# A two-layer trunk kernel on one core: the low parts of the weights by an adding DMA

## The chip, the core and the metric

The kernel runs on one core of a Trainium2 chip. The metric is the device time of one execution in microseconds (us). Before the change the median of three runs is 747.53 us (746.16 to 750.75). One further execution was profiled; all rows below come from it.

## The reference

A batch of one, 512 positions and a width of 1024 go through two layers in float32. Layer 0 (even) normalises, multiplies by one wide input matrix, and splits the result into a gated chunked MLP, a differential attention of 8 heads and a cross-attention into 256 memory tokens; an output matrix brings the concatenation back to 1024, and it is added to the input. Layer 1 (odd) has the same frame around a convolution of 31 taps, a sparse attention of three branches and a second memory attention:

```python
def even_layer(x, ...):
    h = rms_norm(x, norm_g)
    a_u, a_v, a_g, b_q, b_k, b_v, b_g, m_q, m_g = split_cols(h @ w_in, EVEN_SPLITS)
    y_a = chunked_sgu(jax.nn.gelu(a_u), jax.nn.gelu(a_v), ...) * jax.nn.silu(a_g)
    y_b = o_b.reshape(Bz, S, B_WIDTH) * jax.nn.silu(b_g)
    y_m = memory_attention(m_q, mem_n, ...) * jax.nn.silu(m_g)
    return x + jnp.concatenate([y_a, y_b, y_m], axis=-1) @ w_out
```

## The kernel before, in words

**Products in three parts.** Every large product is made of float32r operands. An operand is split into a high part `h`, the value as float32r holds it, and a low part `l`, the float32 value less `h`. `mm3` (L395 to L398) adds three products: high by high (L396), high by low (L397), low by high (L398). In `proj_T` the weights are the stationary operand and their low part comes third; in `proj_N` the weights are the moving operand and their low part comes second.

**Weight units.** The large weights lie in HBM as 88 units of 128 x 1024 float32 (512 KB), and a 2240-column matrix is read in three more pieces. `load_unit` (L379) takes one page `u` of 2048 words from the pool of weight pages (kind "w" of `arena_r`), and a raw page of 1024 words (three exist); SyncE issues the load (L384), ScalarE copies raw to `h` (L376), and GpSimd subtracts, raw less `h`, into `l` (L377). The raw page comes free after the subtraction. Only the first four units of the program are given VectorE as the subtracting engine (L750, argument `eng`); the other 87 pieces use GpSimd. The same `split` helper with VectorE as default also makes high and low parts of activations, so L376 and L377 have ScalarE and VectorE instructions of other work as well.

**Pages.** There are five weight pages in the dense stages and fewer later (`W_OUT` is 4, `W_ATTN1` is 2, and free pages are lent between weights and activations). The copy into a page waits until TensorE has done the last product that read it. Pages are dealt out in program order.

**Order of work.** The program is written as streams (Python generators) that `merge` (L702) interleaves in given shares: attention with projections, gates, convolution taps and output products. A planner (`schedule_with_timeline_sim=True`, L1387) then sets the order in which each engine gets its instructions, by its own estimate of durations and by priority. On the chip each engine works through its own list in order, and waits on semaphores. GpSimd's list also holds the inverse square roots of the norms (`rstd`, L370 and L372), the scaling of some softmax rows (L570) and the additions of one convolution tile (L1257). VectorE's list holds the other three convolution tiles (L1259), score reductions (L925), softmax scaling (L572), norm arithmetic (L511, L883, L957) and the low parts of activations (L377).

Of the kernel before, what the change touches and what calls it, by code (L numbers as in the profile page):

```python
# [26 lines left out]
AF = mybir.ActivationFunctionType  # L27
ALU = mybir.AluOpType
AX = mybir.AxisListType
ADD, SUB, MUL, MAX = ALU.add, ALU.subtract, ALU.mult, ALU.max  # L30
# [255 lines left out]
def emit(ctx, tc, nc, D, out):  # L286
# [8 lines left out]
    def SC():  # L295
        return Scope(arenas)
# [8 lines left out]
    V, A, G, mm = nc.vector, nc.scalar, nc.gpsimd, nc.tensor.matmul  # L305
    dma = nc.sync.dma_start
    act = A.activation

    def f32(t):
        return t.bitcast(F32)  # L310
# [64 lines left out]
    def split(src, h, l, eng=None):  # L375
        act(h, src, AF.Copy)  # L376
        (eng or V).tensor_tensor(l, src, f32(h), SUB)  # L377

    def load_unit(sc, dram, w=DM, eng=None):  # L379
        u = sc([P, 2, DM], F32R, "w")  # L380
        h, l = u[:, 0, :w], u[:, 1, :w]
        with SC() as rs:
            raw = rs([P, w], F32, "raw")
            dma(raw, dram)  # L384
            split(raw, h, l, eng or G)
        return h, l

    def load(sc, name):
        i, n = UIDX[name]
        return [load_unit(sc, D["wall"][i + j]) for j in range(n)]  # L390
# [41 lines left out]
    def unit_parts(wsc, part, n, eng=None):  # L432
        w = []
        for nk, src in part:
            h, l = load_unit(wsc, src, nk * n, eng)
            w += [(h[:, j * n:(j + 1) * n], l[:, j * n:(j + 1) * n]) for j in range(nk)]
        return w
# [959 lines left out]
```

## Time and profile before

| what | value |
|---|---|
| median of three runs | 747.53 us (746.16 to 750.75) |
| the profiled execution | 751.36 us, span of its instructions 749.7 us |
| TensorE products, busy | 683.0 us (91%) |
| VectorE, busy | 533.0 us (71%) |
| GpSimd, busy | 390.3 us (52%) |
| ScalarE, busy | 365.9 us (49%) |
| mean granted TensorE clock | 0.959 of full speed |
| read from HBM | 57.46 MB |

The span is the time from the first to the last instruction; 1.7 us of the profiled execution lie around it. Busy time of an engine that others do not wait for costs nothing. TensorE's products are pipelined, so that their busy times overlap a little, and 91% is not a peak rate.

### The profile page before, as it was taken

The numbers are of one execution on the slowest core, as the hardware profiler recorded it, in microseconds if no ns is written. First come the engines' busy times: TensorE is split into PE (matmuls) and PEld (weight loads), VectorE is DVE, ScalarE is ACT, GpSimd is POOL, SyncE is SP. The second block draws the span as 40 slices with busy tenths as digits, with TensorE's granted clock in tenths as the row PEclk, the third lists the DMA queues.
The fourth block names the chain that finished last, engine by engine and source line by source line (L and its number), as shares of the span: only waits on it lengthen the run. The fifth ranks groups of instructions, "written<-read, shape, count | busy, mean of one in ns | idle before, by whom it ended". The sixth has DMA issues, their size and how long they took to land.

```text
span 749.7 us, 10913 instructions
## 1 busy us (share of the span) xinstructions
PE 683.0 (91%) x3819; PEld 577.0 (77%) x3819; DVE 533.0 (71%) x1216; ACT 365.9 (49%) x819; POOL 390.3 (52%) x343
## 2 busy tenths in 40 slices
PE   4999999999999889999999799895579989899997
PEld 3889998778898668887887688684457878787866
DVE  4507798678778696745479829999636875979883
ACT  5245346465655674534254754322412745675651
POOL 3376985645356686417375586983233422442540
PEclk9999999999999998999999899998598999999999
DMA  8442244552222542112232110032021100110112
GB/s 304 156 150 75 65 145 118 167 161 92 71 85 86 180 154 108 66 57 66 80 126 73 56 57 29 29 115 83 0 84 57 57 29 29 57 57 30 57 66 75
DMA packets 22375, 66.55 MB, mean 89 GB/s; under 512 B 3504, under 2 KB 3760, under 8 KB 22320
## 3 DMA queue, kind: packets, MB, share of 16 engines
q1 hardware_dynamic: 22320, 65.86, 26.8%
q8 instruction: 30, 0.49, 0.3%
q14 instruction: 25, 0.20, 0.1%
HBM read 57.46 MB, written 2.10 MB: 79 GB/s over the span
## 4 chain that ended last, share of the span: by engine, by line
PE 60%; DVE 27%; POOL 4%; issue 4%; ACT 4%; DMA 1%; SPq 0%; ACTq 0%; DVEq 0%; POOLq 0%
PE banks L397 15%; PE banks L396 15%; PE banks L398 15%; DVE banks L1259 5%; PE banks L393 4%; DVE arena_r L377 4%; PE banks L923 2%; PE banks L1211 2%; POOL arena_f L372 2%; DVE arena_f L572 2%; POOL arena_r L377 2%; DVE arena_f L925 2%; ACT arena_r L376 2%; DMA arena_f<-in_wall_dram 1%; PE banks L961 1%
## 5 line engine op out<-in xcount | busy, mean ns | idle before, releaser
L396 PE MATMUL banks<-arena_r 128*128 128x512 f32 (+2 forms) x784 | 295.1, 382 | 11.3 <-DVE arena_f L473 3.3
L397 PE MATMUL banks<-arena_r 128*128 128x512 f32 (+2 forms) x784 | 295.3, 378 | 5.9 <-POOL arena_r L377 5.1
L377 POOL TENSOR_TENSOR arena_r<-arena_f,arena_r 128x1024 fp32r<-128x1024 f32 (+2 forms) x87 | 211.9, 2444 | 170.6 <-ACT arena_r L376 170.1
L398 PE MATMUL banks<-arena_r 128*128 128x512 f32 (+2 forms) x784 | 294.0, 377 | 0.0
L396 PEld LDWEIGHTS banks<-arena_r 128*128 128x128 f32 x784 | 151.9, 194 | 37.8 <-ACT arena_r L376 4.6
L397 PEld LDWEIGHTS banks<-arena_r 128*128 128x128 f32 x784 | 152.8, 195 | 31.0 <-POOL arena_r L377 6.6
L398 PEld LDWEIGHTS banks<-arena_r 128*128 128x128 f32 x784 | 152.4, 194 | 23.8 <-POOL arena_r L377 0.4
L376 ACT ACTIVATE arena_r<-arena_f 128x1024 fp32r<-128x1024 f32 (+2 forms) x131 | 110.3, 854 | 97.9 <-PE banks L398 31.8
L393 PE MATMUL banks<-const,arena_f 128*128 128x128 f32 x507 | 84.8, 286 | 34.1 <-DVE arena_f L521 12.4
L393 PEld LDWEIGHTS banks<-const,arena_f 128*128 128x128 f32 x507 | 63.6, 148 | 46.8 <-DVE arena_f L521 13.5
L376 ACT ACTIVATE arena_r<-banks 128x512 fp32r<-128x512 f32 (+1 forms) x112 | 57.9, 533 | 68.0 <-PE banks L393 42.9
L377 DVE TENSOR_TENSOR arena_r<-banks,arena_r 128x512 fp32r<-128x512 f32 (+1 forms) x112 | 67.2, 607 | 29.5 <-ACT arena_r L376 28.9
L925 DVE CUSTOM_DVE_ANT_0 arena_f<-banks,const 128x512 f32<-128x512 f32 (+3 forms) x128 | 60.4, 482 | 17.9 <-PE banks L923 14.0
L372 POOL TENSOR_TENSOR arena_f<-arena_f,const 128x4 f32<-128x4 f32 (+3 forms) x60 | 68.4, 1142 | 3.7
L570 POOL TENSOR_SCALAR arena_f<-arena_f 128x256 f32<-128x256 f32 (+3 forms) x48 | 30.8, 646 | 73.1 <-DVE arena_f L1190 27.6
L1259 DVE SCALAR_TENSOR_TENSOR banks<-arena_f,const,banks 128x482 f32<-128x482 f32 (+14 forms) x90 | 66.0, 733 | 1.5
L954 ACT ACTIVATE arena_f<-arena_f 128x512 f32<-128x512 f32 (+3 forms) x64 | 35.8, 560 | 41.7 <-DVE arena_f L925 41.4
L923 PE MATMUL banks<-arena_r 128*128 128x256 f32 (+7 forms) x192 | 51.2, 337 | 2.6 <-DVE arena_f L925 2.5
L370 POOL TENSOR_SCALAR arena_f<-arena_f 128x4 f32<-128x4 f32 (+3 forms) x60 | 18.0, 300 | 61.4 <-DVE arena_f L494 23.9
L653 DVE TENSOR_TENSOR arena_f<-arena_f,banks 128x512 f32<-128x512 f32 x40 | 27.3, 683 | 31.5 <-PE banks L398 31.3
L1188 ACT ACTIVATE arena_f<-arena_f 128x256 f32<-128x256 f32 (+3 forms) x64 | 35.6, 559 | 26.7 <-DVE arena_f L925 26.4
L1257 POOL TENSOR_TENSOR arena_f<-arena_f 128x482 f32<-128x482 f32 (+29 forms) x30 | 38.0, 1268 | 2.7 <-ACT arena_f L1256 1.2
(175 smaller groups left out, 840.1 us busy)
## 6 DMA issues: line engine op xcount, KB each, us to landing
arena_f<-in_wall_dram SPq DMA_DIRECT2D x88, 512.0 KB, 3.3
arena_r<-arena_r SPq DMA_DIRECT2D x96, 64.0 KB, 2.0
arena_f<-in_x_dram SPq DMA_DIRECT2D x7, 512.0 KB, 4.6
arena_f<-in_w_dram SPq DMA_DIRECT2D x4, 512.0 KB, 4.0
out_dram<-arena_f SPq DMA_DIRECT2D x8, 256.0 KB, 2.0
arena_f<-in_norms_dram SPq DMA_DIRECT2D x3, 512.0 KB, 4.5
arena_f<-in_mem_dram SPq DMA_DIRECT2D x2, 512.0 KB, 3.2
arena_f<-in_wqb_dram SPq DMA_DIRECT2D x2, 420.0 KB, 3.2
```

Source lines behind the costliest of these rows:

```text
L372: G.tensor_tensor(r, v, mhalf[:parts, :n], ALU.pow)
L376: act(h, src, AF.Copy)
L377: (eng or V).tensor_tensor(l, src, f32(h), SUB)
L393: nc.tensor.transpose(o, i, ident[:k, :k])
L396: mm(o, lh, rh, start=first, stop=False)
L397: mm(o, lh, rl, start=False, stop=False)
L398: mm(o, ll, rh, start=False, stop=last)
L923: mm(t[:, a % per, :], q, k[:, :w], start=b == 0, stop=b == len(qk) - 1)
L925: V.tensor_tensor_reduce(e[a], t[:, a % per, :], cmask[:, S - w:], -1.0, -NEG, ADD, ALU.min, nm[:, a:a + 1])
L954: act(e[m], e[m], AF.Exp, bias=nm[:, m:m + 1], scale=-1.0, accum_out=l[:, i, m:m + 1])
L1257: G.tensor_tensor(acc[:, z:], acc[:, z:], t[:, z:], ADD)
L1259: V.scalar_tensor_tensor(acc[:, z:], hc[:, :S - z], cw[:, f, k:k + 1], acc[:, z:], MUL, ADD)
```

## The change

Where no engine is named, the low part is no longer subtracted. ScalarE writes `h`, reads it again and writes its negative into `l`; then GpSimd's queue issues a DMA that reads the same 512 KB of the weights from HBM once more and adds them onto `l`. The raw page is read by one instruction only, the copy to `h`. The four units that name VectorE keep the old way.

```diff
@@ load_unit @@
             raw = rs([P, w], F32, "raw")
             dma(raw, dram)
-            split(raw, h, l, eng or G)
+            if eng is not None:
+                split(raw, h, l, eng)
+            else:
+
+                act(h, raw, AF.Copy)
+                act(l, f32(h), AF.Copy, scale=-1.0)
+                G.dma_start(l, dram, accum_op=ADD)
         return h, l
```

## Rows read from the trace of the kernel before

**Rows 1.** The page: TensorE's busy time, and the chain that ended last, by engine.
```profile
PE 683.0 (91%) x3819; PEld 577.0 (77%) x3819; DVE 533.0 (71%) x1216; ACT 365.9 (49%) x819; POOL 390.3 (52%) x343
PE 60%; DVE 27%; POOL 4%; issue 4%; ACT 4%; DMA 1%; SPq 0%; ACTq 0%; DVEq 0%; POOLq 0%
```
**Rows 2.** Groups: line, engine, out<-in, count | busy us, mean ns | idle before, releaser.
```profile
L377 POOL TENSOR_TENSOR arena_r<-arena_f,arena_r 128x1024 fp32r<-128x1024 f32 (+2 forms) x87 | 211.9, 2444 | 170.6 <-ACT arena_r L376 170.1
...
L376 ACT ACTIVATE arena_r<-arena_f 128x1024 fp32r<-128x1024 f32 x88 | 92.9, 1057 | 83.2 <-PE banks L398 30.5 <-issue 21.6 <-PE banks L397 14.2
```
**Rows 3.** Waits, whole span: waiter <- what ended it: us, times, longest us.
```profile
ACT arena_r L376 <- PE banks L398: 42.1, 24, 9.9
...
ACT arena_r L376 <- DMA arena_f<-in_wall_dram: 13.0, 6, 5.2
...
PE banks L397 <- POOL arena_r L377: 5.1, 4, 2.1
```
**Rows 4.** Waits of SyncE's queue, whole span.
```profile
SPq L384 <- POOL arena_r L377: 457.9, 63, 36.1
```
**Rows 5.** L377 on GpSimd from 60 to 240 us: ns min/median/max, first and last start.
```profile
L377 POOL TENSOR_TENSOR arena_r<-arena_f,arena_r x23: 2357/2398/2482, 61.6 to 237.4; 128x1024 fp32r<-128x1024 f32 x23
```
**Rows 6.** The same from 240 to 385 us: its wait, and who waited for it.
```profile
L377 POOL TENSOR_TENSOR arena_r<-arena_f,arena_r x24: 1378/2400/2967, 244.5 to 384.3; 128x1024 fp32r<-128x1024 f32 x21, 128x840 fp32r<-128x840 f32 x2, 128x560 fp32r<-128x560 f32 x1
...
  ACT arena_r L376: 47.8, 12
...
  PE banks L397: 2.4, 2
```
**Rows 7.** The same from 545 to 750 us: its wait, and who waited for it.
```profile
L377 POOL TENSOR_TENSOR arena_r<-arena_f,arena_r x18: 2355/2394/2594, 545.5 to 721.0; 128x1024 fp32r<-128x1024 f32 x18
...
  ACT arena_r L376: 72.3, 15
...
  PE banks L397: 2.7, 2
```
**Rows 8.** Timeline of ScalarE: start us, us, instruction [idle before <-releaser].
```profile
660.89 1.04 ACT L376 ACTIVATE arena_r<-arena_f 128x1024 fp32r<-128x1024 f32 x1
...
672.06 1.06 ACT L376 ACTIVATE arena_r<-arena_f 128x1024 fp32r<-128x1024 f32 x1 [0.31 <-PE banks L397]
```
**Rows 9.** Timeline of GpSimd, the same stretch.
```profile
662.01 2.48 POOL L377 TENSOR_TENSOR arena_r<-arena_f,arena_r 128x1024 fp32r<-128x1024 f32 x1 [2.28 <-ACT arena_r L376]
```
**Rows 10.** Timeline of TensorE, two products of one unit in a dense stage.
```profile
47.49 0.39 PE L398 MATMUL banks<-arena_r 128*128 128x512 f32 x1
...
47.72 0.39 PE L396 MATMUL banks<-arena_r 128*128 128x512 f32 x1
```
**Rows 11.** Timeline of GpSimd from 240 us: three subtractions in a row.
```profile
253.40 7.12 POOL L377 TENSOR_TENSOR arena_r<-arena_f,arena_r 128x1024 fp32r<-128x1024 f32 x3 [5.99 <-ACT arena_r L376]
```
**Rows 12.** Two VectorE lines by source: ns min/median/max.
```profile
L957 DVE SCALAR_TENSOR_TENSOR arena_f<-arena_f,const x32: 204/219/2093, 105.6 to 266.4; 128x1 f32<-128x1 f32 x32
...
L883 DVE TENSOR_TENSOR arena_f<-arena_f x16: 407/424/2589, 74.4 to 131.9; 128x256 f32<-128x256 f32 x16
```
**Rows 13.** Groups of VectorE, the same two lines.
```profile
L957 DVE SCALAR_TENSOR_TENSOR arena_f<-arena_f,const 128x1 f32<-128x1 f32 x32 | 17.3, 542 | 0.7
...
L883 DVE TENSOR_TENSOR arena_f<-arena_f 128x256 f32<-128x256 f32 x16 | 14.0, 874 | 6.2 <-POOL arena_f L372 6.2
```
**Rows 14.** Timeline of VectorE, one long L883.
```profile
103.10 1.85 DVE L883 TENSOR_TENSOR arena_f<-arena_f 128x256 f32<-128x256 f32 x1
```
**Rows 15.** Timeline of GpSimd, the same moment.
```profile
102.26 2.40 POOL L377 TENSOR_TENSOR arena_r<-arena_f,arena_r 128x1024 fp32r<-128x1024 f32 x1
```
**Rows 16.** The unit loads (L384) by source: issue ns, and us to landing.
```profile
L384 SPq DMA_DIRECT2D arena_f<-in_wall_dram x88: 327/328/848, 2.2 to 714.0; - x88
...
DMA to landing us min/median/max: 2.7/3.3/10.0
```
**Rows 17.** The page: SyncE's DMA queue, packets, MB, share of 16 engines.
```profile
q1 hardware_dynamic: 22320, 65.86, 26.8%
```

## The prediction, on record before the changed kernel ran

> **What bounds the kernel now.** I read the page's engine totals and its chain first. TensorE is busy for 91% of the span and holds 60% of the chain; VectorE holds 27%, GpSimd and ScalarE 4% each [rows 1]. So GpSimd is no bound in itself: what it finishes matters where TensorE needs a low part at once, and what it disturbs matters on VectorE.
>
> Next I read the groups of the split. GpSimd makes 87 low parts of about 2.4 us each, 211.9 us together, and before them it idled 170 us for the copy L376; that copy takes 1.06 us [rows 2]. The waits say what holds the copy: TensorE's last product on the page 24 times, for 42.1 us, a raw load only 6 times, for 13.0 us [rows 3]. A weight unit is thus made at the turn of its page, and its latency from the turn to the end of the low part is what TensorE has to bridge. TensorE itself waited 5.1 us for L377 [rows 3].
>
> The third view is L377 by stretch. From 60 to 240 us there are 23 subtractions and nobody waited for one: five pages turn, and a new unit stands behind several finished ones [rows 5]. From 240 to 385 us there are 24; for 12 of them GpSimd stood waiting for the copy, and TensorE waited twice, 2.4 us [rows 6]. From 545 us on there are 18, 15 of them with GpSimd waiting, and TensorE waited twice, 2.7 us [rows 7]. The late stretch has the least spare.
>
> **One late unit, step by step.** A page turns at 660.89 and again at 672.06, 11.2 us later [rows 8]. The low part ends at 662.01 + 2.48 = 664.49, so 3.6 us of the turn are latency [rows 8, 9]. The unit's 24 products of 512 columns need 24 x 0.23 = 5.5 us, by the spacing of two products in a dense stage [rows 10]. That leaves 11.2 - 5.5 = 5.7 us of other products (attention, convolution sums) to fill the latency with. With 3.6 us to fill, the cover is enough; it ends at 5.7.
>
> **What the change removes.** The 87 subtractions leave GpSimd [rows 2]. With them goes something that the busy shares do not show: a VectorE instruction that works on SBUF alone is held until the subtraction ends. L883 normally takes 0.42 us; the one at 103.10 took 1.85 and ended with the subtraction begun at 102.26 [rows 14, 15]. By count times median, L957 should take 32 x 0.219 = 7.0 us and L883 16 x 0.424 = 6.8; they take 17.3 and 14.0, so 17.5 us are such holds on these two lines alone [rows 12, 13]. 17.5 of VectorE's 533.0 us is 3.3%; of the 27% x 750 = 202 us that VectorE has on the chain, 3.3% is 6.6. Other lines have holds too, so I take **9 us back**, with 0 to 14 as bounds (0 if the DMA's issue holds VectorE likewise).
>
> The raw page comes free after the copy instead of after the subtraction. SyncE's queue waited 457.9 us for L377 [rows 4], so loads will start earlier by 2.5 us or more. The copy seldom waits for a load [rows 3], so I price this at nothing; its cover is the page wait, and without that the gain is at most the 13.0 us.
>
> **What it adds on ScalarE.** 87 passes of 1.06 us are 92 us; ScalarE goes from 366 to 458 of 750 us, still half idle [rows 1, 2]. Whatever is queued behind a pass comes 1.06 us later: evictions and exponentials for which VectorE and TensorE wait. ScalarE's 4% of the chain are 30 us; a quarter more work there would be 7.5; half of it falls into its waits. I take **4 us lost**, 0 to 8.
>
> **What it adds as transfers.** 87 DMAs bring 87 x 0.524 = 46 MB more from HBM. SyncE's queue moved 65.86 MB in 26.8% of 16 engines' time [rows 17]; at that price a stream of 46 MB is 19% more, and with the old value read as well some 37%, so the engines are not full. Their issue is in GpSimd's queue. It stands there until ScalarE's second pass ends, and the norms' inverse roots and softmax scalings behind it stand with it; as GpSimd now waits for L376 in the same place [rows 2], this is 1.1 us longer per wait, against a 2.4 us subtraction that is gone. The issue itself has no row here; SyncE's takes 0.33 us [rows 16] and the subtraction that it replaces 2.4, and anything between shortens GpSimd's queue. Price: nothing.
>
> **The adding transfer itself** has no row: no DMA of this kernel adds. Its nearest row is the plain load of the same bytes, 3.3 us median from issue to landing, 10.0 at worst [rows 16]. It must also read what it adds to. By the queue's rate 512 KB cost 0.268 x 750 / 65.86 x 0.524 = 1.6 us on 16 engines [rows 17]; 3.3 + 1.6 = 4.9 us, which I take. Low end 3.3 (the second read is hidden), high end 10.0.
>
> Latency then: copy 1.06, second pass 1.06, two hand-overs of 0.1 (661.93 to 662.01 [rows 8, 9]), transfer 4.9, together 7.2 us instead of 3.6. Less the cover of 5.7, 1.5 us per exposed unit are left. Exposed are the 15 late units [rows 7]; of the 12 from 240 to 385 us one in three, since subtractions come there three in a row [rows 11] and transfers of three pages overlap: 4. (15 + 4) x 1.5 = **28 us lost**. Before 240 us nothing: five pages cover 3.6 us more, as nobody waits there now.
>
> **Sum.** 751.4 (profiled execution) + 28 + 4 - 9 = 774.4; the median of the runs is 3.8 below the profiled one, so **771 us**.
>
> A rule of the Trainium skill prices this transfer lower: "DMA: Bandwidth & Descriptors", section "Anatomy of one DMA — SWDGE (gpsimd) path", gives about 2.0 us plus bytes over 436 GB/s, an estimate of 3.2 us for 512 KB; no run so far shows such a DMA. By it the latency is 5.5 us, inside the cover, and the first rival below is what happens.
>
> The same page, section "SWDGE vs HWDGE vs iDMA", says that GpSimd writes the descriptors into SBUF, where VectorE's two-port modes can lock it out. No row of this case shows that; held up by one instruction as long as L883's 0.42 us [rows 12] the transfer would come that much later, an estimate, and the sum would be 8 us higher.
>
> **Rivals.**
> *Faster: the latency stays covered.* If the transfer lands within 3.4 us of its issue, 1.06 + 1.06 + 0.2 + 3.4 = 5.7 is the cover and no unit is exposed; VectorE's holds and TensorE's 5.1 us behind L377 go. 751.4 - 9 - 5 = 737, less 3.8: 733 to 738 with ScalarE's cost. For it: the plain load takes 3.3, and ScalarE and the DMA engines have room. Against: a second read of the same size, and a turn that was sampled once. Chance 0.20.
> *No change: holds returned and latency exposed cancel,* 743 to 752, at some 0.3 us exposed per unit (0.3 x 19 + 4 = 9.7 against 9). Chance 0.14.
> *Slow adding.* At the 10.0 us of the worst load the latency is 12.3, 6.6 us exposed for 19 units, 125 us: 751.4 + 125 + 4 - 9 - 3.8 = 868. For it: a read, an addition and a write of the same bytes may not overlap as a copy's do. Chance 0.08.
> *The planner.* It orders each engine's list by its own idea of the new steps. If it believes that the low part comes sooner than it does, TensorE's list has the products too early and even the 5.7 us of cover is lost; if it knows the latency, it may find more cover than one turn shows. The trace cannot tell which; it widens the forecast's own case.
>
> **Numbers.** Forecast case: slower, 753 to 815 (a transfer of 6.6, two plain loads, exposes 3.2 x 19 = 61 us and gives 804; the planner adds the rest), chance 0.58. The range **732 to 815** takes in this case, no change and the faster rival, and leaves out the slow adding and some of the edges. A time within 1% of 747.5 is what the measurement cannot tell from no change. Faster 0.20, same 0.14, slower 0.66.
>
> **What would show it.** In the changed profile: the adding DMA's time to landing near 4.9 us; ScalarE near 458 us busy and GpSimd near 180; L883 and L957 back at their medians; TensorE's waits at L397 and L398 now named after the DMA, mostly after 545 us, some 20 to 30 us in all; nothing lost before 240 us. The forecast is wrong if the transfer lands within 3.4 us, or if TensorE does not wait for it although it lands late, since then the cover was larger than the one turn says; it is far too low if waits for it show in the first third.

## The result

The changed kernel takes 819.23 us (median; 815.07 to 824.71). The ratio to the kernel before is 1.0958, with a 95% interval of 1.0911 to 1.1006. The direction was forecast, the size was not: about 72 us were lost where 24 were expected, and 819 lies above the range.

The page of the changed kernel answers to [rows 1] and [rows 17]; the DMA issues give KB each and the median us from issue to landing.

```profile
span 822.9 us, 11078 instructions
...
PE 715.5 (87%) x3819; PEld 595.7 (72%) x3819; DVE 474.1 (58%) x1216; ACT 445.1 (54%) x906; POOL 257.4 (31%) x343
...
q0 software_dynamic: 12528, 45.19, 30.8%
q1 hardware_dynamic: 22320, 65.86, 24.4%
...
arena_f<-in_wall_dram SPq DMA_DIRECT2D x88, 512.0 KB, 4.6
arena_r<-in_wall_dram POOLq DMA_DIRECT2D x84, 512.0 KB, 7.2
```

Three things stand in it. The adding DMA lands 7.2 us after its issue. VectorE is 59 us less busy with the same 1216 instructions. And TensorE is 32 us *more* busy with the same 3819 products: they ran slower.

What TensorE waited for by name, in the changed kernel (us in total, times, longest), against 5.1 us for the subtraction in [rows 3]:

```profile
PE banks L403 <- DMA arena_r<-in_wall_dram: 31.5, 15, 4.5
PE banks L404 <- DMA arena_r<-in_wall_dram: 16.1, 11, 3.1
...
PE banks L403 <- DMA arena_r<-in_wqb_dram: 4.1, 1, 4.1
```

51.7 us in 27 waits. The same two rows from 571 us on, with half of it:

```profile
PE banks L403 <- DMA arena_r<-in_wall_dram: 13.3, 5, 4.5
PE banks L404 <- DMA arena_r<-in_wall_dram: 12.2, 8, 3.1
```

To see what each stretch lost, I cut both spans at the first products of the same weight units. The columns are the stretch, its length, the busy us (count) of PE, PEld, DVE, ACT, POOL, the granted clock, the DMA share and GB/s. First the kernel before:

```profile
142.00:256.00 114.00, 110.01 (x638) 95.10 (x637) 83.05 (x207) 64.73 (x156) 58.16 (x58) 0.99 0.35 110
256.00:367.00 111.00, 104.98 (x607) 89.42 (x606) 74.43 (x139) 56.70 (x132) 62.83 (x55) 0.95 0.30 101
367.00:488.00 121.00, 112.02 (x589) 92.77 (x590) 93.11 (x156) 59.72 (x118) 82.40 (x68) 0.96 0.18 58
488.00:545.00 57.00, 39.31 (x176) 30.53 (x175) 47.56 (x92) 17.48 (x40) 26.60 (x24) 0.79 0.19 63
545.00:750.00 205.00, 187.05 (x1015) 153.65 (x1015) 145.13 (x389) 99.79 (x243) 69.23 (x56) 0.97 0.16 55
```

Then the changed one:

```profile
143.00:272.00 129.00, 117.84 (x634) 99.83 (x633) 69.75 (x205) 78.86 (x171) 35.30 (x56) 0.91 0.68 168
272.00:401.00 129.00, 109.89 (x610) 92.30 (x609) 63.81 (x135) 73.66 (x151) 36.01 (x55) 0.93 0.69 163
401.00:521.00 120.00, 113.70 (x628) 95.76 (x627) 94.84 (x179) 76.96 (x141) 70.48 (x76) 0.97 0.60 140
521.00:571.00 50.00, 36.10 (x144) 27.44 (x144) 34.28 (x72) 16.53 (x38) 14.68 (x15) 0.80 0.26 64
571.00:823.00 252.00, 207.71 (x1015) 164.85 (x1014) 133.93 (x389) 115.58 (x260) 40.76 (x56) 0.90 0.35 82
```

The last stretch lost 47 us, the two from 143 to 401 lost 15 and 18, the first 1; the two in the middle won 8. There VectorE had been the bound: from 367 to 488 us of the kernel before, 48% of the chain that ended last, added up by engine, is VectorE's, and from 488 to 545 us 73%. The first of these, by line:

```profile
by line: DVE banks L1259 17.6%; PE banks L396 14.2%; PE banks L397 13.8%; PE banks L398 13.0%; DVE arena_f L572 4.8%; DVE arena_f L600 4.1%; DVE arena_r L377 3.6%; issue 2.6%; PE banks L393 2.2%; DVE arena_f L521 1.8%; DVE arena_f L504 1.8%
```

In the changed kernel's last stretch the chain runs through the adding DMA:

```profile
by line: DMA arena_r<-in_wall_dram 27.7%; PE banks L404 12.9%; PE banks L403 12.6%; PE banks L402 11.2%; issue 8.3%; PE banks L399 3.5%; ACT arena_r L390 2.7%; PE banks L1217 2.3%; ACT arena_r L389 1.8%; PE banks L1187 1.6%; ACT arena_r L37
```

In the losing stretches the granted clock fell with the waits. Of the 73 us between the two profiled executions, 47 are more waiting for low parts (51.7 less 5.1) and 32 are TensorE's longer busy time; all its other idling fell by 6. The clock column bears the 32 out: length times what is missing from full clock adds up to 30 us before (114 x 0.01 + 111 x 0.05 + 121 x 0.04 + 57 x 0.21 + 205 x 0.03) and to 59 us after, 29 more, some of it in idle time, where a low clock costs nothing.

One late unit shows both. ScalarE of the changed kernel (start us, us, instruction): the copy to `h` at 666.82, two evictions that the planner put in between, the second pass.

```profile
666.82 1.06 ACT L389 ACTIVATE arena_r<-arena_f 128x1024 fp32r<-128x1024 f32 x1 [1.06 <-PE banks L403]
667.79 0.58 ACT L478 ACTIVATE arena_f<-banks 128x512 f32<-128x512 f32 x1
668.26 0.59 ACT L376 ACTIVATE arena_r<-banks 128x512 fp32r<-128x512 f32 x1
668.74 1.06 ACT L390 ACTIVATE arena_r<-arena_r 128x1024 fp32r<-128x1024 f32 x1
```

GpSimd's issue follows 0.3 us after the pass:

```profile
670.09 0.89 POOL L391 DMA_DIRECT2D arena_r<-in_wall_dram  x1 [12.12 <-ACT arena_r L390]
```

and TensorE's first product with this low part starts at 675.50, after 2.05 us of idling for the DMA:

```profile
672.83 0.62 PE L929 MATMUL banks<-arena_r 128*128 128x384 f32 x2 [0.42 <-DVE arena_f L931]
675.50 0.50 PE L404 MATMUL banks<-arena_r 128*128 128x512 f32 x1 [2.05 <-DMA arena_r<-in_wall_dram]
675.84 0.39 PE L402 MATMUL banks<-arena_r 128*128 128x512 f32 x1
676.07 0.39 PE L403 MATMUL banks<-arena_r 128*128 128x512 f32 x1
...
676.85 0.63 PE L403 MATMUL banks<-arena_r 128*128 128x512 f32 x1
677.28 0.63 PE L404 MATMUL banks<-arena_r 128*128 128x512 f32 x1
```

From the copy to the low part's first use are 8.7 us; the unit of [rows 8, 9] had its low part ready after 3.6. And 1.3 us after the wait the spacing of the products goes from 0.23 to 0.43 us: the lower of the two clock levels (1.2 instead of 2.4 GHz), for the next seven. Before it TensorE had idled 2.05 us for the DMA and, shortly before that, 0.42 us for VectorE. Such waits are paid once as idling and once more as slow products.

The relief of VectorE came as forecast. The two lines of [rows 12, 13] in the changed kernel (L889 is the former L883, L963 the former L957):

```profile
L963 DVE SCALAR_TENSOR_TENSOR arena_f<-arena_f,const 128x1 f32<-128x1 f32 x32 | 8.6, 270 | 0.7
...
L889 DVE TENSOR_TENSOR arena_f<-arena_f 128x256 f32<-128x256 f32 x16 | 6.7, 420 | 2.0 <-POOL arena_f L372 1.7
```

8.6 and 6.7 us where it was 17.3 and 14.0: nearly all of the holds are gone.

The raw loads are not where the time went. They landed later than before (4.6 us at the median instead of 3.3), but ScalarE's copies waited for them 10.8 us in all, less than the 13.0 of [rows 3].

### The profile page after: what moved, and what is told of

Same layout as the page of the kernel before. It is cut to its first block, busy times and chain, and to the rows that moved or that the text cites. A ratio compares the mean times of both kernels' runs of the same rounds, so it can differ in the third digit from the quotient of the medians.

```text
span 822.9 us, 11078 instructions
## 1 busy us (share of the span) xinstructions
PE 715.5 (87%) x3819; PEld 595.7 (72%) x3819; DVE 474.1 (58%) x1216; ACT 445.1 (54%) x906; POOL 257.4 (31%) x343
## 5 line engine op out<-in xcount | busy, mean ns | idle before, releaser
L403 PE MATMUL banks<-arena_r 128*128 128x512 f32 (+2 forms) x784 | 303.5, 388 | 35.7 <-DMA arena_r<-in_wall_dram 31.5
L404 PE MATMUL banks<-arena_r 128*128 128x512 f32 (+2 forms) x784 | 301.9, 386 | 16.1 <-DMA arena_r<-in_wall_dram 16.1
L402 PE MATMUL banks<-arena_r 128*128 128x512 f32 (+2 forms) x784 | 300.3, 389 | 7.6 <-DVE arena_f L1075 1.8
L403 PEld LDWEIGHTS banks<-arena_r 128*128 128x128 f32 x784 | 156.8, 200 | 65.2 <-DMA arena_r<-in_wall_dram 36.4
L404 PEld LDWEIGHTS banks<-arena_r 128*128 128x128 f32 x784 | 157.2, 201 | 43.9 <-DMA arena_r<-in_wall_dram 19.5
L402 PEld LDWEIGHTS banks<-arena_r 128*128 128x128 f32 x784 | 156.3, 200 | 35.3 <-DVE arena_f L479 2.3
L391 POOL DMA_DIRECT2D arena_r<-in_wall_dram x84 | 74.9, 911 | 317.0 <-ACT arena_r L390 230.7
L389 ACT ACTIVATE arena_r<-arena_f 128x1024 fp32r<-128x1024 f32 (+2 forms) x87 | 90.7, 1047 | 101.1 <-PE banks L404 52.0
L399 PE MATMUL banks<-const,arena_f 128*128 128x128 f32 x507 | 87.4, 291 | 27.4 <-DVE arena_f L417 9.7
L377 DVE TENSOR_TENSOR arena_r<-banks,arena_r 128x512 fp32r<-128x512 f32 (+1 forms) x112 | 67.1, 610 | 58.4 <-ACT arena_r L376 57.3
L390 ACT ACTIVATE arena_r<-arena_r 128x1024 fp32r<-128x1024 f32 (+2 forms) x87 | 90.8, 1047 | 0.7
L372 POOL TENSOR_TENSOR arena_f<-arena_f,const 128x4 f32<-128x4 f32 (+3 forms) x60 | 72.0, 1200 | 4.3
L1265 DVE SCALAR_TENSOR_TENSOR banks<-arena_f,const,banks 128x482 f32<-128x482 f32 (+14 forms) x90 | 66.1, 734 | 1.5
L929 PE MATMUL banks<-arena_r 128*128 128x256 f32 (+7 forms) x192 | 54.0, 352 | 11.3 <-DVE arena_f L931 9.6
L929 PEld LDWEIGHTS banks<-arena_r 128*128 128x128 f32 (+1 forms) x192 | 32.2, 193 | 21.3 <-DVE arena_f L931 17.2
L1263 POOL TENSOR_TENSOR arena_f<-arena_f 128x482 f32<-128x482 f32 (+29 forms) x30 | 40.4, 1347 | 9.2 <-ACT arena_f L1262 7.7
```

What stands on the lines that cost most here:

```text
L372: G.tensor_tensor(r, v, mhalf[:parts, :n], ALU.pow)
L389: act(h, raw, AF.Copy)
L390: act(l, f32(h), AF.Copy, scale=-1.0)
L391: G.dma_start(l, dram, accum_op=ADD)
L399: nc.tensor.transpose(o, i, ident[:k, :k])
L402: mm(o, lh, rh, start=first, stop=False)
```

## The experiments

Ratios are against the kernel before, run beside each on the same chip.

**1. Subtraction again in the last stretch.** A flag chooses between the two ways; it is switched before the loop over the sparse attention.

```diff
+            if eng is not None or not ADDING[0]:
+                split(raw, h, l, eng or G)
+            else:
...
+    ADDING[0] = False
     drain(merge((ahead(d_attn(yD, rev, done), HD), 1.0), (taps, TAPS2),
```

> The adding DMA everywhere but in the last stretch: from the loop over the sparse attention on, the low parts are subtracted by GpSimd again (18 of the 87). Theory W (TensorE's waits for the added low parts, and the lower clock that follows those waits, are the loss, and the last stretch, 252 us instead of 205, has 47 of the 72 us): the time falls by 40 to 50 us, to 770 to 780, and the last stretch's clock is back at 0.96 or more. Rival P (the loss is that the planner laid out the whole program worse once it knew the new steps): the last stretch stays slow or the loss moves forward, 800 or more. Rival T (the added 46 MB of transfers slow everything): the 18 late units are a fifth of them, 805.

Measured: 771.68 us, ratio 1.0333 (1.0270 to 1.0397). The last stretch in this run:

```profile
564.00:769.00 205.00, 186.66 (x1020) 153.52 (x1018) 142.94 (x389) 102.52 (x245) 66.31 (x56) 0.98 0.18 60
```

205 us and a clock of 0.98, as before the change; TensorE's waits for added low parts in this stretch fell from 25.5 to 2.4 us. By the trace 16 units went back to GpSimd, not 18: two of the stretch were still made by the adding DMA. So 16 of 87 units carried 47 of the 72 us. Theory W held. As the planner laid out this stretch anew too, the run by itself does not part the latency from the order of the lists; run 4 does.

**2. The adding DMA in the middle stretch alone.**

```diff
     glu = c_glu()
+    ADDING[0] = True
...
+    ADDING[0] = False
     drain(merge((ahead(d_attn(yD, rev, done), HD), 1.0), (taps, TAPS2),
```

> The other way round: the adding DMA only for the units of the middle stretch (convolution inputs, second memory queries, key, value and query projections of layer 1, the memory part of the output product), GpSimd's subtraction everywhere else. In the changed kernel this stretch, in which VectorE is the bound, took 50 + 120 us where before it took 57 + 121. Theory H (VectorE no longer held by subtractions: the relief of 10 us and more in this stretch is real): 735 to 740, faster than before. Rival C (the stretch only caught up a delay made earlier, because VectorE had been running ahead): 745 to 750, no change. Rival W (even here TensorE waits for the DMA, 6 us seen): 750 to 755.

Measured: 740.25 us, ratio 0.9907 (0.9874 to 0.9940): about 1% faster than before. By the trace 25 of the 87 pieces came by the adding DMA. Its stretches, cut at the same units:

```profile
367.00:475.00 108.00, 106.30 (x601) 90.10 (x599) 82.01 (x158) 71.38 (x133) 62.11 (x66) 1.00 0.55 132
475.00:532.00 57.00, 41.10 (x183) 33.01 (x180) 46.85 (x94) 21.72 (x45) 21.68 (x26) 0.82 0.41 102
532.00:736.00 204.00, 185.93 (x1017) 152.99 (x1015) 142.95 (x389) 102.52 (x245) 66.30 (x56) 0.97 0.19 60
```

108 us instead of 121, VectorE 82 us busy instead of 93, and nothing lost later. The chain in the first of these stretches is now TensorE's for 82% and VectorE's for 7%, where VectorE had 48%:

```profile
by line: PE banks L404 24.0%; PE banks L402 23.7%; PE banks L403 23.3%; DMA arena_r<-in_wall_dram 4.8%; PE banks L399 3.7%; POOL arena_f L1263 3.5%; DVE arena_f L517 2.3%; PE banks L604 1.8%; PE banks L603 1.7%; PE banks L590 1.4%; PE banks
```

The profiled executions lie 13 us apart (738.29 and 751.36) and the medians 8, so the stretch shows where the gain is rather than its size. The relief is real where VectorE holds TensorE back; it was not a delay caught up. What no run here parts is VectorE's freedom from holds and GpSimd's own list, which is 25 subtractions shorter, and the new order of the lists.

**3. The negated part first.** It is made straight from the raw page, and the DMA goes out before the copy.

```diff
-                act(h, raw, AF.Copy)
-                act(l, f32(h), AF.Copy, scale=-1.0)
+                act(l, raw, AF.Copy, scale=-1.0)
                 G.dma_start(l, dram, accum_op=ADD)
+                act(h, raw, AF.Copy)
```

> The negated high part is made straight from the raw page (rounding the raw value and negating it gives the same number), before the high part, and the DMA is issued before the second pass: the same 87 passes and the same 87 DMAs, but each low part comes about 1.06 us sooner. Theory W (latency): 26 waits of TensorE each 1.06 us shorter are 28 us, and the clock gives some 10 more: 780 to 795. Rival A (the added pass costs as load on ScalarE, whatever its place): no change, 815 to 822. Rival P (planner): anything, without a fall of TensorE's waits for the DMA.

Measured: 831.28 us, ratio 1.1126 (1.1060 to 1.1192), slower than the changed kernel. TensorE's waits there:

```profile
PE banks L402 <- DMA arena_r<-in_wall_dram: 33.4, 16, 6.0
PE banks L403 <- DMA arena_r<-in_wall_dram: 25.2, 10, 3.8
```

58.6 us, not less than 47.6: theories W and A missed. The profiled executions (826.09 and 824.71 us) differ by 1.4 us only, so that the traces tell little about the 12 us between the medians; but they tell why the waits did not shrink. The landing of the DMA in the last stretch, in this run and then in the changed kernel:

```profile
DMA to landing us min/median/max: 5.0/7.0/9.0
```
```profile
DMA to landing us min/median/max: 5.0/5.4/9.0
```

The DMA went out sooner and landed later by as much: added up over the units of this stretch, page turn to landing is 9.5 us at the median against 9.3. Rival P's sign, no fall of the waits, did come, but not because the planner placed the products with the low part earlier: between a page's turn and that use TensorE's list holds no less work in this stretch than in the changed kernel. Why the transfers took longer I did not find out. What the run shows is that a shorter chain in the program need not shorten the waits on the chip.

**4. A plain DMA in place of the adding one.**

```diff
-                G.dma_start(l, dram, accum_op=ADD)
+                G.dma_start(l, dram)
```

> The changed kernel with a plain DMA in place of the adding one: the same issue on GpSimd's queue, the same bytes from HBM, but the old value is not read and nothing is added (the low parts are left out, l holds the raw weights). Theory S (the addition is what makes the transfer long): median from issue to landing falls from 7.2 us to 4 to 5, each of some 26 waits of TensorE gets 1 to 2 us shorter and the clock gives back as much as half of that: 770 to 795. Rival G (any DMA issued by GpSimd takes that long): landing above 6.5, time 812 to 822. Theory of the prediction (the second read costs 1.6 us): landing 5.6, 785 to 800.

Measured: 765.95 us, ratio 1.0228 (1.0173 to 1.0282). The DMA by source (ns of the issue, us to landing: min/median/max):

```profile
L391 POOL DMA_DIRECT2D arena_r<-in_wall_dram x84: 527/585/767, 24.0 to 739.1; - x84
...
DMA to landing us min/median/max: 3.5/4.7/8.8
```

TensorE's waits for it:

```profile
PE banks L403 <- DMA arena_r<-in_wall_dram: 13.2, 10, 2.1
PE banks L404 <- DMA arena_r<-in_wall_dram: 3.1, 4, 1.2
```

The same two rows of the changed kernel:

```profile
L391 POOL DMA_DIRECT2D arena_r<-in_wall_dram x84: 848/880/1842, 24.4 to 796.2; - x84
...
DMA to landing us min/median/max: 5.0/7.2/14.0
```

The addition costs 1.5 us at the least and 2.5 at the median; the issue itself is 0.3 longer. These 2.5 us per unit are worth 53 us of time (819 less 766), more than the prediction's whole loss; TensorE's waits for these DMAs fell from 47.6 to 16.3 us. This is the cleanest pair of the series: instruction by instruction the lists of TensorE, ScalarE, VectorE and GpSimd are the same in both traces, so nothing of the difference is the planner's. Between the two profiled executions, 58 us apart, TensorE idled 36 us less and was busy 22 us less with the same products, at a granted clock of 0.953 instead of 0.927:

```profile
PE 693.6 (91%) x3819; PEld 582.5 (76%) x3819; DVE 473.8 (62%) x1216; ACT 444.6 (58%) x906; POOL 230.7 (30%) x343
```

Theory S held, and the time fell even below its range.

**5. The second pass alone.** GpSimd adds the raw page onto the negated part; no DMA adds.

```diff
-                G.dma_start(l, dram, accum_op=ADD)
+                G.tensor_tensor(l, raw, f32(l), ADD)
```

> ScalarE's second pass alone: it still writes the negated high part, but GpSimd then adds the raw page onto it, and no DMA does. Against the kernel before this has 87 passes of 1.06 us more and low parts 1.06 us later, and nothing else. The prediction's term for the pass was 4 us: 751. Theory W: the 19 exposed units stay within the cover of 5.7 us (latency 4.7), 747 to 755. Rival A (the pass itself is a main cost): 765 to 785.

Measured: 779.68 us, ratio 1.0438 (1.0388 to 1.0487), the rival's range. TensorE waited by name for the low parts

```profile
PE banks L403 <- POOL arena_r L391: 6.7, 6, 2.3
```

only 6.7 us, so most of these 32 us are not waits for a low part by name. Half of them lie in the last stretch: 220 us at a granted clock of 0.94, instead of 205 at 0.97. Two readings remained: load on ScalarE, or a longer way to the low part around which the planner laid a worse list. Run 9 tells them apart.

**6. Products with the low part last.** In `proj_T` the sixteen products with the high part go first.

```diff
             for k in range(KT):
-                mm3(p, wh[:, k, :], wl[:, k, :], hs[0][k // 4][:, k % 4, :], hs[1][k // 4][:, k % 4, :],
-                    k == 0, k == KT - 1)
+                for x in range(2):
+                    mm(p, wh[:, k, :], hs[x][k // 4][:, k % 4, :], start=k + x == 0, stop=False)
+            for k in range(KT):
+                mm(p, wl[:, k, :], hs[0][k // 4][:, k % 4, :], start=False, stop=k == KT - 1)
```

> The changed kernel, but the projections with stationary weights (37 of the 87 units, 8 of them in the last stretch) do their sixteen products with the high part first and the eight with the low part last: 16 x 0.23 = 3.7 us more cover in each such unit. The sum of each output gets the same addends in another order. Theory W (exposed latency, 4.2 us for each of 11 late units, and the clock after it): most of the late loss goes, 775 to 795. Rival P (the planner puts other work elsewhere and the waits stay): 805 or more.

Measured: 777.11 us, ratio 1.0406 (1.0344 to 1.0469). The last stretch:

```profile
570.00:774.00 204.00, 187.77 (x1012) 155.97 (x1012) 130.15 (x388) 113.86 (x257) 38.54 (x55) 0.95 0.41 99
```

204 us, with every low part still made by the adding DMA, and TensorE's waits for them here down from 25.5 to 7.9 us:

```profile
PE banks L403 <- DMA arena_r<-in_wall_dram: 6.9, 4, 2.2
PE banks L437 <- DMA arena_r<-in_wall_dram: 1.0, 1, 1.0
```

By the trace 34 units have the new order, 8 of them in this stretch. More cover inside the unit does for this stretch what going back to the subtraction did in run 1. That is the second sign, by another edit, that latency beyond the cover was its loss.

**7 and 8. The same order of products in the kernel before, and with run 2.**

> Control: the same order of products in the kernel before, with GpSimd's subtraction. There the list covers 3.4 us of a latency of 4.5 in the last stretch, and TensorE waited 5.1 us in all for low parts. Theory W: 738 to 746, a small gain. Rival: no change, 746 to 750, since those waits were not what held the end.

> The adding DMA in the middle stretch alone (740 us median), and in addition the products with the low part last. If both gains are real and add up: 730 to 737. If the second gives nothing where GpSimd subtracts: 738 to 743.

Measured: 749.50 us, ratio 1.0013 (0.9980 to 1.0046), and 756.35 us, ratio 1.0112 (1.0066 to 1.0157). In the kernel before, where TensorE waited 5.1 us for low parts, the order is worth nothing: the rival of run 7 held. Together with run 2 it takes that gain back and 8 us more. Both expectations of run 8 missed. TensorE waited 11.0 us for added low parts there and 5.9 in run 2; where the rest of its 16 us goes I did not find out.

**9. The second pass as load alone.** The kernel before, with 87 passes that write a page nobody reads.

```diff
-            split(raw, h, l, eng or G)
+            act(h, raw, AF.Copy)
+            (eng or G).tensor_tensor(l, raw, f32(h), SUB)
+            if eng is None:
+                act(junk[:, :w], f32(h), AF.Copy, scale=-1.0)
```

> The kernel before, with ScalarE's second pass as load alone: after the copy it also writes the negated high part into a page of bfloat16 that nobody reads, while GpSimd subtracts from the copy as before. 87 passes of about 1.06 us more on ScalarE, but no low part has to wait for them. Theory L (the pass cost 32 us in the run with GpSimd's addition because it lies in the low part's latency): 748 to 756. Rival A (ScalarE's load costs, by what is queued behind it): 770 to 785.

Measured: 752.94 us, ratio 1.0070 (1.0043 to 1.0097). The added passes in the list of ScalarE's groups:

```profile
L389 ACT ACTIVATE junk<-arena_r 128x1024 bf16<-128x1024 f32 (+2 forms) x87 | 90.8, 1043 | 0.5
```

91 us of load cost 5 us. The other 27 of run 5 are put down to the place of the pass, between the copy and the low part, and to the lists that the planner laid around it; the runs do not part these two.

**10. Run 2 without the narrow pieces.** `w < DM` takes the subtraction as well. The edit is against run 2.

```diff
-            if eng is not None or not ADDING[0]:
+            if eng is not None or not ADDING[0] or w < DM:
```

> The adding DMA in the middle stretch alone, but without the three narrow pieces of the second memory query, for one of which TensorE waited 2.8 us there: 19 units by DMA, 68 by subtraction. Theory W: 736 to 740, a little under the 740 of the run with all 22. Rival (the wait only moves, VectorE is the bound there): 739 to 743.

Measured: 737.97 us, ratio 0.9877 (0.9831 to 0.9922), the lowest median of all. It is not told apart from run 2. By the trace 22 units came by DMA and 65 by subtraction, where run 2 had 25 and 62: the expectation counted three DMA pieces too few in both.

## Why the size was wrong, point by point

Put in a row, the runs split the loss by the change's own parts: the pass as load 5 us (run 9), its place in the low part's way 27 more (run 5 less run 9), a plain DMA instead of GpSimd's work 14 back (run 4 less run 5), the addition 53 (the change less run 4). The last of these has the same lists on both sides; the others are differences between programs that were each planned anew, so each of them is good to some us at best.

- **What the chain of the kernel was:** right. TensorE held it, and GpSimd mattered only by what it finished late and what it disturbed.
- **The holds on VectorE:** the mechanism was right (L889, L963). The size, 9 us of time, is of the right order but was not measured alone: run 4 has 14 less than run 5 but has transfers in place of subtractions besides, runs 2 and 10 are 8 and 10 below their kernel before with only 25 and 22 pieces changed, and in the changed kernel all other idling of TensorE fell by 6.
- **The load on ScalarE, 4 us:** right, 5 measured.
- **The earlier raw loads, at nothing:** right, by the 10.8 us against 13.0.
- **The latency, 7.2 us, and its cover, 5.7 us:** this step failed. The transfer was priced at 4.9; it took 5.4 in the last stretch and 7.2 over the whole span. The two passes were counted back to back, but in the unit above 0.86 us of evictions lay between them, and the issue came 0.3 us after the pass instead of 0.1. Added up for the late units, copy to landing took 9.3 us at the median. The cover was read from [rows 8] as one page's turn, but the first copy there names no product of TensorE as what it waited for, so that the 11.2 us are not shown to be one turn. I summed the spacings of the products that stand in TensorE's list between a page's turn and the unit's first product with the low part, for the late units whose page was last a weight page: about 3.4 us of work before and 5.3 after. That the new list came near the 5.7 is luck. The real time over the same products was about 4.5 and 9.6 us. So some 4 us per late unit were uncovered, not 1.5. The named waits for the low part fill half of that (25.5 us in 13 waits, 2.0 each); other waits and slow products fill the rest.
- **What an exposed us costs:** this was put at nothing; the sum has no term for the clock. TensorE's clock dropped to its lower level after the waits, the products behind them took 0.43 instead of 0.23 us, and the same 3819 products kept TensorE busy 32 us longer. With the measured 47 us of waits in place of 28 the sum gives 789; the 32 us bring it to 822. That this comes within 3 us of the 819 is partly luck, since the other terms are known to some us only.
- **The number of exposed units, 19:** TensorE waited 27 times. "Nothing before 240 us" was wrong: four of the waits, 8.0 us, lie there, and the stretch from 143 us lost 15. The prediction had named waits in the first third as the sign that it would be far too low. There the DMA engines were now busy for 0.68 of the time instead of 0.35. That nobody waited for a low part before said that there was some spare, not how much.
- **The issue, at nothing:** it took 0.85 to 0.93 us in 82 of the 87 cases and at most 1.84. A hold-up of each by some 0.4 us, priced at 8 us, does not show in it.
- **The Trainium skill's price**, "DMA: Bandwidth & Descriptors", section "Anatomy of one DMA — SWDGE (gpsimd) path", an estimate of 3.2 us: the plain GpSimd DMA came near it at its fastest (3.5), the adding one never did (5.0 at the least). The rival that hung on it fell.
- **The rivals:** the slow adding (10 us, 868) pointed at the addition, the dearest part, with too high a price; why an addition takes longer than a copy no run shows. No change and faster did not happen for the whole kernel. The faster rival's relief is what runs 2 and 10 kept, where VectorE was the bound and units had spare.

Still open: how much of run 5's 27 us the planner's new lists hold and how much the chip's latency, why the transfers of run 3 took longer, and where run 8 lost.

## What to carry to other kernels

A step in the way of double-buffered weights is to be priced by its latency against the work that the list really holds between a page's turn and its use, and that at every stage, since one of them can decide: here the last took 47 of 73 us. Count TensorE's clock with each exposed wait: here the slow products made the bill of the waits about two thirds as large again (32 on 47 us, and 22 on 34 between run 4 and the changed kernel). And a change that trades an engine's time for latency can be right in the stage where that engine's neighbour is the bound and wrong elsewhere: here the same edit is 1% faster on 22 of 87 units and 10% slower on all.

## What was not expected of the hardware

An adding DMA of 512 KB issued by GpSimd landed after 5.0 us at the least and 7.2 at the median, a plain one from the same queue after 3.5 and 4.7; its issue held GpSimd for 0.88 us against 0.59. With 45 MB of such DMAs beside them, SyncE's plain loads of the same size went from 3.3 to 4.6 us (4.1 beside as many plain ones). A GpSimd subtraction on SBUF held a VectorE instruction on SBUF until it ended: L883 took up to 2.59 us with the subtractions and 0.43 at most with the DMAs in their place. VectorE's 1216 instructions took 533 us with the subtractions and 474 with the DMAs, while its convolution line, which works on PSUM (`banks`, L1259 before and L1265 after), took 66.0 and 66.1.
